# The attention mask's corner set before its load, and a dense tile's experts copied by VectorE ahead of the next search

## The chip, the cores and the metric

One core of one Trainium2 chip runs the whole program. The metric is the device time of one execution in microseconds (us), the median of three runs. The profile shows one further execution, recorded by the hardware profiler.

## The reference, cut to what matters

One layer of a streaming encoder over 512 positions of width 1024 (fp32):

```python
z = rmsnorm(x) @ w_in                    # x_lru, gate, q, k, v
y_a = rg_lru(x_lru) * gelu(gate)         # conv, gates, scan over positions
y_b = chunk_attention(q, k, v, rel_bias) # 8 heads; a chunk of 64 sees itself and 8 before it
x = x + concat(rmsnorm(y_a), rmsnorm(y_b)) @ w_out
x = x + memory_cross_attention(...)      # 4 heads, 256 memory tokens
# PEER: 8 heads, 128 x 128 = 16384 single-neuron experts, 16 picked per head
v1, i1 = top_k(q1 @ keys1, 16); v2, i2 = top_k(q2 @ keys2, 16)
top, pos = top_k(v1[:, None] + v2[None, :], 16)
idx = (i1 * 128 + i2)[pos]; g = softmax(top)
out = (g * gelu(x @ expert_u[idx])) @ expert_v[idx]
return rmsnorm(x + out)
```

In the attention the scores of a block of 128 queries get the relative-position bias added, and a key of a later chunk gets -1e30. In a tile of 128 queries by 512 keys that is one corner: the first 64 queries against the last 64 keys.

## The kernel before

All positions lie in four tiles of 128. Every fp32 product is made of three matmuls on a value's high and low part; the weights are split on the chip (a copy on ScalarE, L169, and a subtraction on VectorE, L207; for some of the U weights the low part is made by a ScalarE copy, L175, and an accumulating DMA from the POOL queue, L176).

A planner turns the program text into one fixed queue for each engine: it takes the instruction that stands first by its priority (the place in the text, moved forward by `tc.high_priority(offset=...)`) among those that its own model of time holds ready. `tc.issue_after(ins)` ties what a block traces, on the engine of `ins`, to come behind `ins` in that queue. On the chip each engine runs its queue strictly in order, and waits where an input or a buffer isn't there. From the last stage on (`tc.manual_schedule()`) the order is that of the text.

**The mixing stage** follows the string MIX_ORDER. Three letters bear on the change. "B" is `load_bias(h)` (L558 to L561): the bias of head h is loaded from HBM into a tile bt of 128x512 by one DMA on the SP queue (L560), and VectorE then writes -1e30 into the corner `[0:64, 448:512]` (L561), so that this memset waits for the load. "S" is `scores(h)`: two matmuls for each query tile (L573, L574) and one VectorE operation that adds bt and takes the maximum (L575). "R" is `lru_rec(n)` (L532 to L537), a row of VectorE operations of the recurrence on what ScalarE left from the gates (L520 to L524). The value projection `z_v` keeps four PSUM banks (pv) until ScalarE and VectorE have taken high and low part of each out of it (L106, L107).

**The expert stage.** The first query tile, t = 0, is done by gathering its experts. Tiles 1 to 3 are dense: for each token a table of 128x128 weights is built, one for each pair of key indices, and the experts are then computed for all tokens. `second_level(t, tp)` is the search that picks the 16 experts of each head for tile t: it is a generator, and each `yield` ends a step. The first step makes the candidate sums (L1001 to L1005); then come maxima and their positions (L1013 to L1023), an exponential on ScalarE (L1028), two passes over eq (L1050 to L1063), and the weights gF (L1068 to L1070). At its end PE turns the picked indices and weights into a PSUM bank pt (L1082, L1084). ScalarE copies the indices out to ij (L1089) and the scaled weights to gg[:, :, 0] (L1090), and VectorE makes gg's low part from both (L1091).

Search 1 runs beside eight blocks of the first expert product (`mm1_parts`, 24 matmuls each, L112 to L114). Then tile_ = 1, 2, 3 are built, 16 groups each: VectorE makes hot (L1125, from ij) and wei (L1129, from hot and gg), each with two buffers; PE multiplies them in two halves of 8 matmuls (L1136), ScalarE takes each half out into a stage (L1138), and a stage goes to DRAM (Wd, L1148). Between the halves PE gets parts of further U blocks by a fixed rate, and the text takes two steps of the search for tile_ + 1 in every three halves (`level`, offset OFF2 = 10). At a later point gathers, the second product (L1241) and the rest of the U blocks run by hand-written order.

Of the kernel before, what the change touches and what calls it, by code (L numbers as in the profile page):

```python
# [16 lines left out]
AF = mybir.ActivationFunctionType  # L17
OP = mybir.AluOpType
# [37 lines left out]
GS = float(2 ** 15)  # L56
# [20 lines left out]
def layer(ctx, tc, a, out, upto=99, dbg=None):  # L77
    nc = tc.nc
    dbg = dbg or {}
    V, A, PE, SP, PL = nc.vector, nc.scalar, nc.tensor, nc.sync, nc.gpsimd  # L80
# [12 lines left out]
    def bank(name="bk"):  # L93
        return psum.tile([128, 512], F32, name=name, tag="bk")
# [242 lines left out]
    def s(name, dt=F32):  # L337
        return s1.tile([128, S], dt, name=name, tag="s")
# [216 lines left out]
    BT, PR, PT, PO = {}, {}, {}, {}  # L555
    LAST = []

    def load_bias(h):  # L558
        BT[h] = s("bt")
        SP.dma_start(BT[h], a["bias"][h])  # L560
        V.memset(BT[h][0:64, 448:512], NEG)  # L561

    def scores(h):
        b, hs = divmod(h, 2)
        q, kh, kl = QK[b][hs], QK[4 + b][hs], QK[4 + b][2 + hs]
        mx = sm.tile([128, TT], F32, name="mx")
        su = sm.tile([128, TT], F32, name="su")
        P = PR[h] = [s("p") for t in range(TT)]
        for qt in range(TT):
            n = (qt + 1) * 128  # L570
            qs = slice(qt * 128, (qt + 1) * 128)
            ps = bank()
            PE.matmul(ps[:, :n], q[:, qs], kh[:, :n], start=True, stop=False)  # L573
            PE.matmul(ps[:, :n], q[:, qs], kl[:, :n], start=False, stop=True)  # L574
            V.tensor_tensor_reduce(P[qt][:, :n], ps[:, :n], BT[h][:, 512 - n:], scale=1.0, scalar=LOW,  # L575
                                   op0=OP.add, op1=OP.max, accum_out=mx[:, qt:qt + 1])
        V.tensor_scalar(mx, mx, -1.0, None, op0=OP.mult)
        for qt in range(TT):
            n = (qt + 1) * 128
            with tc.issue_after(LAST[-1]) if LAST else ExitStack():  # L580
                e = A.activation(P[qt][:, :n], P[qt][:, :n], AF.Exp, bias=mx[:, qt:qt + 1], accum_out=su[:, qt:qt + 1]).ins
        if h == 3 or h == 4:
            LAST[:] = [e] * 4
        return su
# [91 lines left out]
    for n in range(4):  # L676
# [3 lines left out]
    kinds = {"q": z_qk, "k": lambda n: z_qk(4 + n), "v": z_v, "gt": z_gate, "mk": mem_k, "mv": mem_v}  # L680
    steps = {
        "B": load_bias, "G": lru_gates, "R": lru_rec, "A": lambda n: lru_act(), "L": lru_scan,
        "W": lambda n: kinds[MIX_W[n][0]](MIX_W[n][1]),
        "S": lambda h: su.update({h: scores(h)}), "P": lambda h: probs(h, su[h]), "T": turn, "V": values,
# [164 lines left out]
    with tc.tile_pool(name="hx", bufs=2) as hx:  # L849
        ho = []  # L850
        for c in range(NCH):
            t = hx.tile([128, S], F32, name="ht")
# [36 lines left out]
    def mm1_next():  # L889
        ahead[0] += 1  # L890
        return mm1_parts(ahead[0] - 1)
# [77 lines left out]

    Wd = dram.tile([128, 8 * DT, NE, 16], F32)  # L970
    HK = [128, 8, 16]
    SEL = {}

    class Rooms:

# [20 lines left out]
    def second_level(t, tp):  # L996
# [89 lines left out]
        ij = tp.tile([128, 16, 2, 8], F16, name="ij", bufs=2)  # L1086
        gg = tp.tile([128, 16, 2, 8], F16, name="gg", bufs=2)
        pv = pt.rearrange("p (s g k) -> p s g k", s=4, k=8)
        A.copy(ij.rearrange("p g s k -> p s g k"), pv[:, 0:2])  # L1089
        A.activation(gg[:, :, 0], pv[:, 2], AF.Copy, scale=GS)  # L1090
        V.scalar_tensor_tensor(gg[:, :, 1], pv[:, 2], GS, gg[:, :, 0], op0=OP.mult, op1=OP.subtract)  # L1091
        SEL[t] = ij, gg

    def hurried(steps, offset):
        while True:
            with tc.high_priority(offset=offset) if offset else ExitStack():
                if next(steps, 0) == 0:
                    return
            yield

    with (tc.tile_pool(name="wg", bufs=2) as wg, tc.tile_pool(name="st", bufs=2, side="right") as stages,
          tc.tile_pool(name="wx", bufs=1) as W.more):
        parts, owed = iter(()), 0.0
        done = 0
        for k, _ in enumerate(hurried(second_level(1, tp), OFF1)):
            while ahead[0] < LAG and done < (k + 1) * U_MID / 15 and done < U_MID:
                done += 1
                for _ in mm1_next():
                    pass
        for tile_ in range(1, TT):  # L1110

            blocks = U_TILE[tile_ - 1] if tile_ < DT else LAG - SPARE - ahead[0]
            rate = blocks * NCH / 16
            level = hurried(second_level(tile_ + 1, tp) if tile_ < DT else iter(()), OFF2)
            ij, gg = SEL.pop(tile_)
            for q in range(8):
                tb = (tile_ - 1) * 8 + q
                stage = stages.tile([128, NE, 16], F32, name="stage", tag="stage")
                for t8 in range(0, 16, 8):
                    gr = (q * 16 + t8) // 8  # L1120

                    pairs = lambda x: x[:, gr].rearrange("p s (q k) -> p (s q) k", k=2)
                    F8 = [128, 8, NE, 2]
                    hot = wg.tile(F8, F16, name="hot")
                    V.tensor_tensor(hot, io2[:, None].to_broadcast(F8), pairs(ij)[:, :, None].to_broadcast(F8),  # L1125
                                    op=OP.is_equal)
                    wei = wg.tile(F8, F16, name="wei")
                    W8 = [128, 2, 4, NE, 2]
                    V.tensor_mul(wei.rearrange("p (s q) n k -> p s q n k", s=2),  # L1129
                                 hot[:, None, 0:4].to_broadcast(W8),  # L1130
                                 gg[:, gr].rearrange("p s (q k) -> p s q k", k=2)[:, :, :, None].to_broadcast(W8))
                    for t4 in (0, 4):
                        ps = bank()
                        for k in range(t4, t4 + 4):
                            for part in range(2):
                                PE.matmul(ps[:, (k - t4) * 128:(k - t4 + 1) * 128], hot[:, 4 + k // 2, :, k % 2],  # L1136
                                          wei[:, 4 * part + k // 2, :, k % 2], start=part == 0, stop=part == 1)
                        A.activation(stage[:, :, t8 + t4:t8 + t4 + 4], ps.rearrange("p (t i) -> p i t", t=4),  # L1138
                                     AF.Copy, scale=1.0 / GS)
                        if (q * 4 + (t8 + t4) // 4) % LEVEL[1] < LEVEL[0]:  # L1140
                            next(level, 0)
                        owed += rate / 2
                        while owed >= 1:
                            owed -= 1
                            if next(parts, 0) == 0 and ahead[0] < LAG - SPARE:
                                parts = mm1_next()
                                next(parts)
                SP.dma_start(Wd[:, tb], stage)  # L1148
            for _ in level:
                pass  # L1150
        for _ in parts:
            pass
        while ahead[0] < LAG - SPARE:
            for _ in mm1_next():
                pass
        W.more = None
        W.fill(W.used + 3)
# [139 lines left out]
    order.enter_context(tc.manual_schedule())  # L1297

    level = second_level(0, Rooms(gp))

    def level_steps(n):
# [114 lines left out]
```

## Time and profile before

| | us |
|---|---|
| median of 3 runs | 1620.49 |
| lowest, highest | 1618.95, 1622.12 |
| the profiled execution | 1620.74 |
| its span, first to last instruction | 1618.7 |

The page of the profile gives busy times by engine, the span in 40 slices, and the groups of instructions. PE is TensorE's matmul, PEld its weight load, DVE VectorE, ACT ScalarE, POOL GpSimd, SP SyncE. In a timeline a row gives the start, the duration, the engine, the line, the operation, out<-in, shapes and a count; the bracket holds the idle time of the engine just before it and what ended that. Where an operation starts before the one ahead of it has ended, both overlap in the engine's pipeline. The granted clock of TensorE (PEclk) is 1.00 at 2.4 GHz and 0.50 at 1.2 GHz.

### The profile page before, as it was taken

The numbers are of one execution on the slowest core, as the hardware profiler recorded it, in microseconds if no ns is written. First come the engines' busy times: TensorE is split into PE (matmuls) and PEld (weight loads), VectorE is DVE, ScalarE is ACT, GpSimd is POOL, SyncE is SP. The second block draws the span as 40 slices with busy tenths as digits, with TensorE's granted clock in tenths as the row PEclk, the third lists the DMA queues.
The fourth block names the chain that finished last, engine by engine and source line by source line (L and its number), as shares of the span: only waits on it lengthen the run. The fifth ranks groups of instructions, "written<-read, shape, count | busy, mean of one in ns | idle before, by whom it ended". The sixth has DMA issues, their size and how long they took to land.

```text
span 1618.7 us, 23682 instructions
## 1 busy us (share of the span) xinstructions
PE 1590.8 (98%) x8554; PEld 1402.6 (87%) x8554; DVE 1259.5 (78%) x2444; ACT 748.8 (46%) x1192; POOL 458.6 (28%) x335
## 2 busy tenths in 40 slices
PE   9999999999998999999999999999999999999998
PEld 7788878888887989899999999999999999988886
DVE  6778884655899986887777777777777777788887
ACT  6578753446545666553333333333333333333335
POOL 0111000001101100003454455454445454553330
PEclk9999999999999999999999999999999999999999
DMA  7454442127867789877999889889898998999994
GB/s 247 143 136 130 139 157 92 66 66 212 201 150 179 229 254 299 286 248 265 323 311 319 313 309 320 294 317 317 302 328 304 319 315 298 324 326 335 315 333 156
DMA packets 156933, 403.73 MB, mean 249 GB/s; under 512 B 13856, under 2 KB 64672, under 8 KB 153744
## 3 DMA queue, kind: packets, MB, share of 16 engines
q1 hardware_dynamic: 111744, 242.10, 43.5%
q0 software_dynamic: 44928, 159.86, 32.0%
q8 instruction: 67, 1.10, 0.3%
q14 instruction: 50, 0.41, 0.1%
q10 hardware_dynamic: 144, 0.26, 0.0%
HBM read 348.69 MB, written 29.36 MB: 234 GB/s over the span
## 4 chain that ended last, share of the span: by engine, by line
PE 87%; DVE 7%; DMA 3%; ACT 3%; issue 1%; SPq 0%; POOL 0%; ACTq 0%; DVEq 0%; POOLq 0%
PE acc L1241 33%; PE bk L112 15%; PE bk L114 15%; PE bk L113 15%; PE bk L1136 2%; DMA Wd<-stage 2%; PE om L113 1%; PE om L114 1%; PE om L112 1%; PE bk L932 1%; PE pv L112 1%; PE pv L113 1%; DVE wl L207 1%; PE pv L114 1%; DVE hot L1125 1%
## 5 line engine op out<-in xcount | busy, mean ns | idle before, releaser
L169 ACT CAST wh<-w 128x1024 fp32r<-128x1024 f32 x326 | 342.5, 1051 | 305.2 <-PE acc L1241 193.4
L112 PE MATMUL bk<-hH,wh 128*128 128x384 f32 (+1 forms) x1096 | 383.0, 349 | 0.0
L114 PE MATMUL bk<-hH,wl 128*128 128x384 f32 (+1 forms) x1096 | 374.7, 342 | 0.0
L113 PE MATMUL bk<-hL,wh 128*128 128x384 f32 (+1 forms) x1096 | 374.2, 341 | 0.0
L207 DVE TENSOR_TENSOR wl<-w,wh 128x1024 fp32r<-128x1024 f32 x286 | 348.8, 1221 | 20.7 <-ACT wh L169 20.2
L1170 POOL DMA_INDIRECT g<-in_Un,gidx x128 | 205.6, 1606 | 238.7 <-DVE junk L1177 193.7
L1170 POOL DMA_INDIRECT g<-in_V,gidx x128 | 199.7, 1560 | 226.8 <-DVE gacc L1187 211.4
L1241 PE MATMUL acc<-wh,ph 128*128 128x512 f32 x768 | 239.3, 391 | 0.0
L1241 PE MATMUL acc<-wh,pl 128*128 128x512 f32 x768 | 238.8, 391 | 0.0
L1241 PE MATMUL acc<-wl,ph 128*128 128x512 f32 x768 | 238.7, 390 | 0.0
L1217 DVE TENSOR_TENSOR pl<-act,ph 128x384 fp32r<-128x384 f32 x128 | 71.2, 557 | 185.8 <-ACT ph L1214 185.8
L113 PEld LDWEIGHTS bk<-hL,wh 128*128 128x128 f32 x1096 | 206.4, 188 | 7.0
L112 PEld LDWEIGHTS bk<-hH,wh 128*128 128x128 f32 x1096 | 206.2, 188 | 7.0
L114 PEld LDWEIGHTS bk<-hH,wl 128*128 128x128 f32 x1096 | 206.0, 188 | 4.1
L880 ACT ACTIVATE act<-bk 128x384 f32<-128x384 f32 x128 | 62.9, 491 | 281.0 <-PE bk L114 277.9
L176 POOL DMA_DIRECT2D wl<-w x40 | 34.3, 857 | 485.3 <-ACT wl L175 432.8
L1241 PEld LDWEIGHTS acc<-wl,ph 128*128 128x128 f32 x768 | 144.1, 188 | 31.8 <-DVE wl L207 0.3
L1241 PEld LDWEIGHTS acc<-wh,pl 128*128 128x128 f32 x768 | 144.1, 188 | 31.1
L1241 PEld LDWEIGHTS acc<-wh,ph 128*128 128x128 f32 x768 | 142.9, 188 | 24.3
L1187 DVE SCALAR_TENSOR_TENSOR gacc<-g,gu,gacc 128x1024 f32<-128x1024 f32 x127 | 162.5, 1279 | 1.6 <-DMA g<-in_V,gidx 0.9
L1177 DVE SCALAR_TENSOR_TENSOR junk<-g,htok 128x1024 bf16<-128x1024 f32 x128 | 156.1, 1220 | 1.0
L112 PE MATMUL bk<-oh,wh 128*128 128x512 f32 x280 | 112.4, 402 | 1.4 <-DVE v L107 1.4
(348 smaller groups left out, 2177.8 us busy)
## 6 DMA issues: line engine op xcount, KB each, us to landing
w<-in_V SPq DMA_DIRECT2D x128, 512.0 KB
w<-in_U SPq DMA_DIRECT2D x124, 512.0 KB
Wd<-stage SPq DMA_DIRECT2D x24, 1024.0 KB
wt<-Wd SPq DMA_DIRECT2D x90, 256.0 KB
wl<-w POOLq DMA_DIRECT2D x40, 512.0 KB
w<-in_w_pq SPq DMA_DIRECT2D x16, 512.0 KB
w<-in_w_in SPq DMA_DIRECT2D x14, 512.0 KB
x<-in_xT SPq DMA_DIRECT2D x16, 256.0 KB
```

What stands on the lines that cost most here:

```text
L112: PE.matmul(ps, lh, rh, start=first and c == 0, stop=False)
L113: PE.matmul(ps, lh, rl, start=False, stop=False)
L114: PE.matmul(ps, ll, rh, start=False, stop=last and c == n - 1)
L169: A.copy(wh[:, cs], w[:, cs])
L176: PL.dma_start(wl, w, accum_op=OP.add)
L207: V.tensor_sub(wl[:, cs], w[:, cs], wh[:, cs].bitcast(F32))
L880: A.activation(ACT[e], ps[:, :ND], AF.Gelu_apprx_tanh)
L1170: PL.indirect_dma_start(out=g, out_offset=None, in_=a[table], in_offset=bass.IndirectOffsetOnAxis(ap=gidx[:, k:k + 1], axis=0))
L1177: V.scalar_tensor_tensor(junk, g, 1.0, htok, op0=OP.mult, op1=OP.mult, accum_out=gu[:, st:st + 1])
L1187: V.scalar_tensor_tensor(gacc, g, gu[:, k:k + 1], gacc, op0=OP.mult, op1=OP.add)
L1217: V.tensor_sub(PS[e][1], ACT.pop(e), PS[e][0].bitcast(F32))
L1241: PE.matmul(acc[t, hf], lhs[:, ts], rhs[:, hf * 512:(hf + 1) * 512], start=e == 0 and part == 0, stop=e == NE - 1 and part == 2)
```

## The change

Two edits.

In `load_bias` the memset of the corner comes first in the text, and the load of the bias becomes two DMAs that leave the corner out: columns 0 to 447 of all 128 partitions, and columns 448 to 511 of partitions 64 to 127. No load writes what the memset writes.

In `second_level`, for t = 1 alone, ij and gg[:, :, 0] are copied out of PSUM by VectorE. The low part of gg, the last VectorE operation of the search, is kept in FOUND. The search for tile 2, which the loop of tile 1 takes its steps from, is wrapped in `behind`: its first step is traced as it was, and of all further steps what runs on VectorE is queued behind FOUND[1].

```diff
     def load_bias(h):
         BT[h] = s("bt")
-        SP.dma_start(BT[h], a["bias"][h])
+
         V.memset(BT[h][0:64, 448:512], NEG)
+        SP.dma_start(BT[h][:, :448], a["bias"][h][:, :448])
+        SP.dma_start(BT[h][64:128, 448:512], a["bias"][h][64:128, 448:512])
...
-    SEL = {}
+    SEL, FOUND = {}, {}
...
-        A.copy(ij.rearrange("p g s k -> p s g k"), pv[:, 0:2])
-        A.activation(gg[:, :, 0], pv[:, 2], AF.Copy, scale=GS)
-        V.scalar_tensor_tensor(gg[:, :, 1], pv[:, 2], GS, gg[:, :, 0], op0=OP.mult, op1=OP.subtract)
+        if t == 1:
+
+            V.tensor_copy(ij.rearrange("p g s k -> p s g k"), pv[:, 0:2])
+            V.tensor_scalar(gg[:, :, 0], pv[:, 2], GS, None, op0=OP.mult)
+        else:
+            A.copy(ij.rearrange("p g s k -> p s g k"), pv[:, 0:2])
+            A.activation(gg[:, :, 0], pv[:, 2], AF.Copy, scale=GS)
+        FOUND[t] = V.scalar_tensor_tensor(gg[:, :, 1], pv[:, 2], GS, gg[:, :, 0], op0=OP.mult, op1=OP.subtract).ins
         SEL[t] = ij, gg
...
+    def behind(steps, ins):
+
+        if next(steps, 0) == 0:
+            return
+        yield
+        while True:
+            with tc.issue_after(ins):
+                if next(steps, 0) == 0:
+                    return
+            yield
...
             level = hurried(second_level(tile_ + 1, tp) if tile_ < DT else iter(()), OFF2)
+            if tile_ == 1:
+                level = behind(level, FOUND[1])
```

## Rows read from the trace of the kernel before

**Rows 1.** The page: PE's busy time, share and instructions, and its busy tenths in 40 slices of the span.

```profile
PE 1590.8 (98%) x8554; PEld 1402.6 (87%) x8554; DVE 1259.5 (78%) x2444; ACT 748.8 (46%) x1192; POOL 458.6 (28%) x335
...
PE   9999999999998999999999999999999999999998
```

**Rows 2.** The list of waits of PE over the whole span, the longest: who waited for whom, us in total, times, the longest.

```profile
PE bk L1136 <- DVE wei L1129: 10.2, 5, 8.0
...
PE bk L573 <- DVE v L107: 2.0, 1, 2.0
```

**Rows 3.** Busy time of each engine in stretches of the span, with the granted clock, the DMA engines' share and GB/s as the last three columns.

```profile
80.00:90.00 10.00, 10.00 (x40) 8.17 (x40) 8.29 (x20) 4.62 (x11) 3.73 (x8) 0.83 0.44 123
...
210.00:220.00 10.00, 8.75 (x41) 6.60 (x41) 9.80 (x19) 6.35 (x11) 0.00 (x0) 1.00 0.17 56
...
520.00:530.00 10.00, 6.41 (x43) 6.04 (x44) 9.26 (x11) 4.26 (x6) 0.00 (x0) 0.66 0.56 145
530.00:585.00 55.00, 54.45 (x454) 49.26 (x453) 53.20 (x122) 36.81 (x57) 5.99 (x7) 1.00 0.85 252
585.00:640.00 55.00, 55.00 (x458) 50.17 (x457) 36.35 (x31) 34.08 (x54) 5.14 (x6) 1.00 0.92 286
```

**Rows 4.** VectorE's timeline from 60 to 76 us.

```profile
69.16 0.11 DVE L561 MEMSET bt<- 64x64 f32 x1 [5.77 <-DMA bt<-in_bias]
69.30 0.69 DVE L532 SCALAR_TENSOR_TENSOR ti<-ti,xc 128x512 f32<-128x512 f32 x1
...
74.72 0.48 DVE L107 SCALAR_TENSOR_TENSOR v<-pv,rmix,v 128x256 fp32r<-128x256 f32 x1
```

**Rows 5.** ScalarE's timeline from 60 to 85 us.

```profile
64.65 0.82 ACT L524 ACTIVATE T<-T,sp 128x512 f32<-128x512 f32 x1
...
69.77 0.47 ACT L106 ACTIVATE v<-pv,rmix 128x256 fp32r<-128x256 f32 x1
```

**Rows 6.** PE's timeline from 74 to 85 us (eleven matmuls start from 78.81 to 83.21 us, both counted).

```profile
76.37 0.61 PE L573 MATMUL bk<-qk,qk 128*128 128x512 f32 x1 [2.00 <-DVE v L107]
...
78.81 0.77 PE L112 MATMUL bk<-oh,wh 128*128 128x512 f32 x1 [1.40 <-DVE v L107]
...
83.21 0.47 PE L113 MATMUL bk<-ol,wh 128*128 128x512 f32 x1
...
84.22 0.39 PE L114 MATMUL bk<-oh,wl 128*128 128x512 f32 x1
84.45 0.39 PE L112 MATMUL bk<-oh,wh 128*128 128x512 f32 x1
```

**Rows 7.** What the SP queue's load of the bias (L560) waited for from 55 to 230 us, the longest: us in total, times, the longest.

```profile
SPq L560 <- DVE mo L107: 3.5, 1, 3.5
```

**Rows 8.** VectorE's timeline around the fourth head's mask, 105 to 125 us.

```profile
119.55 0.11 DVE L561 MEMSET bt<- 64x64 f32 x1
...
120.42 0.29 DVE L575 CUSTOM_DVE_ANT_0 p<-bk,bt 128x128 f32<-128x128 f32 x1
```

**Rows 9.** VectorE's timeline from the end of search 1 to the first group of tile 1 (494 to 530 us).

```profile
508.05 0.67 DVE L1013 MAX8 tops<-cand 128x8 f32<-128x80 f32 x4
...
519.86 0.27 DVE L1091 SCALAR_TENSOR_TENSOR gg<-bk,gg 128x128 f16<-128x128 f32 x1
520.05 2.35 DVE L1125 TENSOR_TENSOR hot<-io,ij 128x2048 f16<-128x2048 f16 x2
522.32 2.35 DVE L1129 TENSOR_TENSOR wei<-hot,gg 128x2048 f16<-128x2048 f16 x2
```

**Rows 10.** ScalarE's timeline from 512 to 530 us.

```profile
516.76 1.06 ACT L175 ACTIVATE wl<-w 128x1024 fp32r<-128x1024 f32 x1 [4.41 <-DMA w<-in_U]
517.72 0.35 ACT L1089 CAST ij<-bk 128x256 f16<-128x256 f32 x1
```

**Rows 11.** PE's timeline from 495 to 530 us: the last instruction that fills pt, the last matmul of the eighth U block, and the first and third half of tile 1.

```profile
511.31 0.28 PE L1084 MATMUL bk<-ident,gF 128*128 128x128 f32 x1
...
515.28 0.34 PE L114 MATMUL bk<-hH,wl 128*128 128x384 f32 x1
523.59 1.01 PE L1136 MATMUL bk<-wei,hot 128*128 128x128 f16 x8 [7.97 <-DVE wei L1129]
...
528.84 0.64 PE L1136 MATMUL bk<-wei,hot 128*128 128x128 f16 x8
```

**Rows 12.** PE's timeline, halves of tile 1 further on: the fifth, sixth, seventh and tenth, and the thirtieth.

```profile
533.06 0.64 PE L1136 MATMUL bk<-wei,hot 128*128 128x128 f16 x8
534.66 0.64 PE L1136 MATMUL bk<-wei,hot 128*128 128x128 f16 x8
536.76 0.64 PE L1136 MATMUL bk<-wei,hot 128*128 128x128 f16 x8
...
542.58 0.64 PE L1136 MATMUL bk<-wei,hot 128*128 128x128 f16 x8
...
584.42 0.64 PE L1136 MATMUL bk<-wei,hot 128*128 128x128 f16 x8
```

**Rows 13.** VectorE's timeline, the first and the last operation of search 3 before its weights are turned (530 to 592 us).

```profile
537.92 0.24 DVE L1001 TENSOR_TENSOR cand<-val 128x128 f32<-128x128 f32 x1
...
579.62 0.69 DVE L1063 TENSOR_TENSOR half<-eq 128x1024 f16<-128x1024 f16 x1
```

**Rows 14.** The tile ij: ScalarE's copies into it, duration in ns (lowest, median, highest), first and last start.

```profile
L1089 ACT CAST ij<-bk x3: 355/363/372, 517.7 to 638.4; 128x256 f16<-128x256 f32 x3
```

## The prediction

> **What bounds the kernel now.** I read the page first. PE is busy 98% of the span, 27.9 us short of all of it, and one slice, the thirteenth, falls to 8 tenths [rows 1]. So the time can only come down where PE stands still or runs at the lower clock. The list of PE's waits says where: 10.2 us, of which one wait is 8.0, for VectorE's wei ahead of the first product of the dense tiles, and a wait of 2.0 us for VectorE's v in the mixing stage [rows 2]. Then the stretches: in 80 to 90 us the granted clock is 0.83, in 520 to 530 us 0.66, and 1.00 in the others shown, also in 210 to 220 where PE stood 1.25 us of ten [rows 3]. So the change aims at two places, and I follow each through the timelines of VectorE, ScalarE and PE.
>
> **Edit one, the mask.** VectorE stood 5.77 us until 69.16 because its memset waited for the bias load, and the recurrence (L532 onward) and v's low parts were queued behind it [rows 4]. ScalarE had finished what the first step of the recurrence needs at 64.65 + 0.82 = 65.5 us, and the first high part of v at 69.77 + 0.47 = 70.2 us [rows 5]. With the memset first, no wait for a load stands in VectorE's queue. The recurrence starts as ScalarE delivers, and its operations ahead of v, about 5.4 us in the old order [rows 4], lie under ScalarE's gates. VectorE's first v can then start at about 70.3 instead of 74.72: 4.4 us sooner.
>
> What PE pays now is a wait of 2.00 at 76.37 and one of 1.40 at 78.81, both for v, whose PSUM banks it wants. On top come slow matmuls: eleven starts from 78.81 to 83.21 are 0.44 apart, against 0.23 from 84.22 to 84.45, ten times 0.21 = 2.1 us, and two more at 76.37, 0.4 us [rows 6]. The sum is 5.9 us. Moving v by 4.4 takes the first release from 76.3 to 71.9, ahead of PE, which wants it at 74.4; the second goes from 78.7 to 74.3, and PE, without its first wait and slow clock, would be there at about 75. So both waits and the fall of the clock go. But VectorE and ScalarE are only 4.4 us ahead, so PE may have to give back up to 1.5 us behind this. I take 4.9, half way between 4.4 and 5.9.
>
> What it adds: eight more DMA issues on SP, which nobody waits for, and nothing on VectorE, since the eight memsets of 0.11 [rows 4] only move. As the first writer of its buffer, though, the memset now has to wait for the buffer's last reader, which the load on SP did before. The nearest row is SP's longest such wait, 3.5 us for VectorE's own mo [rows 7]: in VectorE's own queue that is order and costs nothing. Bounds of the edit: a gain of 5.9, and a loss of 3.5 if such a wait for another engine falls on VectorE at a bad place. I stay near the gain, because the row of the longest wait names VectorE itself.
>
> The corner's DMA moves rows of 64 values, 256 bytes each. The mask is needed soonest for the fourth head: its memset found the load landed at 119.55, and the first read came at 120.42 [rows 8]. So there is a margin of 0.87 us or more, and a small second load can eat it at that head alone; I cost it at 0; the upper end is the one wait for a mask that the trace has, 5.77 [rows 4].
> The Trainium skill ("DMA: Bandwidth & Descriptors", the table at its head) asks for 512 B or more for full rate, and says that less is written by read-modify-write; by that the corner's load would be the late one, and the sum would go from 13.0 towards 13.0 - 5.8 = 7.2, instead of losing nothing to it. No row here shows a load of such short rows by itself.
>
> **Edit two, ij and gg on VectorE, search 2 behind.** PE fills pt by 511.31 + 0.28 = 511.6 us, and has no work of its own after the eighth U block, 515.28 + 0.17 = 515.45; then it stands 7.97 us, until 523.59 [rows 11]. In between pt lay waiting. ScalarE's queue held a U weight's low part ahead of ij, and that waited 4.41 us for its load, so that ij came at 517.72 [rows 10]. VectorE meanwhile did search 2 from 508.05 on, and came to gg's low part only at 519.86 [rows 9]. So two queues were late, ScalarE's by 6 us and VectorE's by 8; the change takes away both, and one alone would leave the other.
>
> After it VectorE, done with the first step of search 2 at 508.05, stands until pt is there. Then ij, gg and its low part. ScalarE's ij took 0.35 [rows 10], VectorE's low part, which also reads 128x128 out of pt, 0.27 [rows 9]; so 0.35 + 0.27 + 0.27 = 0.9 us, with 0.8 to 1.4 as ends (1.4 if ij, twice the elements and written out of order, costs thrice the low part). hot starts at 512.5. From the first hot to the first product it was 523.59 - 520.05 = 3.54 us with two hots ahead of two weis [rows 9, 11], and 2.4 if wei comes straight behind its hot (any two of them take 2.35). The first product can then start between 514.9 and 516.0, against PE's 515.45. I take a wait of 0.3 us. So 7.97 - 0.3 = 7.7 us go. The clock fell with the long stand: the first two halves took 528.84 - 523.59 = 5.25 us, and the same pair further on took 536.76 - 533.06 = 3.70 [rows 11, 12], 1.55 lost. A stand of 0.3 doesn't bring that, since 1.25 us in 210 to 220 left the clock at 1.00 [rows 3]. Together 9.2 us.
> The Trainium skill ("VectorE: DVE Perf Modes", Specifications) speaks against the move: ScalarE lies closer to PSUM, and VectorE to SBUF. The rows of this case don't bear that out for size: VectorE's read of pt took 0.27 for 128 columns and ScalarE's 0.35 for 256. If the move doubled the copies' 0.6 us, the sum would be 0.6 us smaller, 12.4 instead of 13.0.
>
> What is pushed back is VectorE's work of 508.05 to 519.86, 11.8 us of search 2 [rows 9]. It now lies among tile 1's groups. There PE is full: four halves take 542.58 - 534.66 = 7.92 us, so a group of two halves 3.96 [rows 12]. VectorE's hot and wei take 2.3 of that [rows 9]. The other 1.7 were filled before too, since VectorE was busy 53.2 of 55 us, but by search 3, from 537.92 to 579.62 [rows 3, 13], whose ij is not copied before 638.4 [rows 14], a whole tile later. Search 2 takes that room, and search 3 goes on to tile 2, where VectorE had 55 - 36.35 = 18.7 us free [rows 3]. The 11.8 us are nine of a search's fifteen steps, 1.3 us each, and the first is done, so 14 steps take 18 us. The room is about 16 x 1.7 = 27 us a tile, part of it for the low parts of U weights, so it fits, though not evenly: two steps are asked for in three halves, 1.33 steps or 1.7 us a group, all of the room for as long as the search lasts. Some groups will come late. Before, from 534.66 to 584.42 the 24 halves took 49.76 where 24 x 1.98 = 47.5 would do: 2.2 us [rows 12]. I expect about 1 us more than that, with -2 to +4 as ends. So edit two gives 9.2 - 1 = 8.2, between 4.5 and 11.
>
> ScalarE loses two copies of 0.6 us together, and POOL's accumulating DMA, which stood behind that ScalarE queue, can only go sooner.
>
> **The sum.** 4.9 + 8.2 = 13.1, taken as 13.0 us. Against the profiled execution, 1620.74 us (span 1618.7 and 2.0 around it), that is 1607.7. The median of the runs is 0.25 lower, and I predict 1608. After the dense tiles PE is full and the order is written by hand, so what is gained ahead of it arrives at the end.
>
> **Rivals.**
> *The mask's gain is given back.* VectorE and ScalarE are busy eight tenths from 80 us on [rows 3], and a mask that is late, or a memset that stands for a buffer, can hold PE again before 200 us. For: the margin at the fourth head. Against: VectorE moves forward as well. Gain 0 to 2 and 8.2: 1610.5 to 1612.5, about 1612.
> *VectorE binds in tile 1 or 2.* If the pushed 11.8 us are put ahead of the next hots by the planner, PE waits where it was fed before, and of the 9.2 only 0 to 3 stay. For: 53.2 of 55 busy. Against: search 3 can wait. With 4.9 from the mask: 1613 to 1616.
> *Slower: the steps of a search delay PE one by one.* They stand 10 places forward in the text's order, so in tiles 1 and 2 a step may be queued ahead of a hot that PE wants. 28 steps of some 1.3 us are at stake; from 0.47 us of each uncovered, 13 us, the change loses, and at 0.6, 17 us, the time is about 1624. Against: before, steps of search 3 lay in the same places and cost 2.2 us in all.
> *It doesn't do what it says.* If the parts of one tile aren't told apart, the loads wait for the memset, and if pt is turned later in PE's queue, nothing is won: 1620.5.
>
> **How the numbers follow.** Forecast, 1605 to 1611: 0.60. Mask given back, about 1612: 0.14. VectorE binds, 1613 to 1617: 0.12. Slower: 0.07. Nothing: 0.07. The range goes from 1604 (all 15 us and part of the old 2.2) to 1615, and leaves out some 0.2. A measurement can tell 0.2%, 3.2 us, from no change. Faster by more: 0.60 + 0.14 + 0.12, less 0.02 at the edge, 0.84. Within: 0.09. Slower: 0.07.
>
> **What would show it.** Right: no wait of VectorE's memset for a load; VectorE's first v near 70; the granted clock 1.00 in 80 to 90 and 520 to 530; VectorE's ij at 511.6 less the 5 us of edit one; the first L1136 less than 1 us behind the last U matmul; search 3 ending after tile 2 has begun. Wrong: PE waiting again for v, for masked scores or for hot in tiles 1 and 2, or VectorE's memset waiting for PE or ScalarE.

## The result and the profile after

The changed kernel took 1609.19 us in the median of 6 runs (1608.58 to 1610.49), the kernel before beside it 1619.74 (1618.72 to 1622.12): a ratio of 0.9933, 95% interval 0.9921 to 0.9946. The profiled execution took 1609.12 us with a span of 1607.1, against 1620.74 and 1618.7 before, so in the traces 11.6 us are to be explained.

The page after, PE's line and its slices, as in [rows 1]; then the list of PE's longest waits, as in [rows 2].

```profile
PE 1588.7 (99%) x8554; PEld 1402.7 (87%) x8554; DVE 1258.9 (78%) x2446; ACT 749.0 (47%) x1190; POOL 459.0 (29%) x335
...
PE   9999999999999999999999999999999999999998
```

```profile
PE bk L1156 <- DVE wei L1149: 3.8, 6, 1.8
PE po L613 <- ACT ph L102: 2.7, 1, 2.7
```

PE's busy time is 2.1 us smaller and the span 11.6: what went is mostly standing (9.5 us), the rest is slow clock. The thirteenth slice is full now. The wait of 8.0 for wei has become six of 1.8 at most, the waits for v are gone from the list, and the wait for ScalarE's ph has grown, from two of 1.0 at most to one of 2.7. The stretches, as in [rows 3]:

```profile
70.00:80.00 10.00, 10.00 (x48) 8.27 (x47) 8.68 (x19) 6.11 (x12) 2.08 (x4) 1.00 0.42 125
80.00:90.00 10.00, 10.00 (x52) 8.43 (x51) 8.65 (x25) 9.19 (x24) 2.06 (x4) 1.00 0.71 177
140.00:150.00 10.00, 7.27 (x49) 6.92 (x48) 6.78 (x12) 9.30 (x22) 1.03 (x2) 0.86 0.50 129
500.00:510.00 10.00, 10.00 (x70) 9.76 (x69) 6.38 (x16) 6.93 (x9) 2.57 (x3) 1.00 0.74 150
510.00:520.00 10.00, 10.00 (x88) 9.12 (x87) 10.00 (x35) 5.77 (x9) 0.86 (x1) 1.00 0.90 219
520.00:530.00 10.00, 9.75 (x79) 8.82 (x76) 10.00 (x43) 8.17 (x12) 1.71 (x2) 1.00 0.98 287
530.00:540.00 10.00, 9.57 (x81) 8.74 (x80) 10.00 (x13) 6.81 (x11) 0.06 (x1) 1.00 0.95 339
540.00:575.00 35.00, 34.07 (x282) 30.45 (x280) 33.30 (x99) 21.88 (x36) 4.23 (x5) 1.00 0.93 261
575.00:600.00 25.00, 23.20 (x179) 21.27 (x178) 24.79 (x30) 16.28 (x26) 1.71 (x2) 0.93 0.77 253
600.00:630.00 30.00, 30.00 (x256) 27.04 (x255) 19.12 (x18) 19.08 (x31) 3.42 (x4) 1.00 1.00 287
```

The two places the change aims at, 80 to 90 and 520 to 530 us, run at a granted clock of 1.00 (0.83 and 0.66 in [rows 3]). VectorE is all but full from 510 to 600 us (1.9 us free of 90), and PE stands 1.8 us between 575 and 600 and runs part of that time at the lower clock.

VectorE's timeline at the head, as in [rows 4], and at the start of tile 1, as in [rows 9]:

```profile
63.14 0.19 DVE L561 MEMSET bt<- 64x64 f32 x2
63.65 0.69 DVE L532 SCALAR_TENSOR_TENSOR ti<-ti,xc 128x512 f32<-128x512 f32 x1 [0.32 <-ACT ti L521]
...
69.97 0.49 DVE L107 SCALAR_TENSOR_TENSOR v<-pv,rmix,v 128x256 fp32r<-128x256 f32 x1
...
506.25 0.42 DVE L1093 CAST ij<-bk 128x256 f16<-128x256 f32 x1 [3.62 <-PE bk L1086]
506.60 0.28 DVE L1094 TENSOR_SCALAR gg<-bk 128x128 f16<-128x128 f32 x1
506.79 1.21 DVE L1145 TENSOR_TENSOR hot<-io,ij 128x2048 f16<-128x2048 f16 x1
507.92 0.28 DVE L1098 SCALAR_TENSOR_TENSOR gg<-bk,gg 128x128 f16<-128x128 f32 x1
508.28 1.21 DVE L1149 TENSOR_TENSOR wei<-hot,gg 128x2048 f16<-128x2048 f16 x1
```

The memset waits for nothing, and v's low part starts 4.75 us sooner than at 74.72. The copy of ij starts as soon as pt is there; one hot and one wei stand between it and the first product. PE's halves, as in [rows 11, 12] (the first and the third half, the thirtieth, three in tile 2), and behind the tiles the first product with V:

```profile
510.08 0.64 PE L1156 MATMUL bk<-wei,hot 128*128 128x128 f16 x8
...
513.78 0.64 PE L1156 MATMUL bk<-wei,hot 128*128 128x128 f16 x8
...
570.43 0.64 PE L1156 MATMUL bk<-wei,hot 128*128 128x128 f16 x8
...
582.82 0.64 PE L1156 MATMUL bk<-wei,hot 128*128 128x128 f16 x8 [1.80 <-DVE wei L1149]
...
585.55 1.08 PE L1156 MATMUL bk<-wei,hot 128*128 128x128 f16 x8
...
588.58 0.64 PE L1156 MATMUL bk<-wei,hot 128*128 128x128 f16 x8
...
709.05 0.63 PE L1261 MATMUL acc<-wh,ph 128*128 128x512 f32 x2
```

In the trace before, the counterparts of the half at 588.58 and of the first product with V:

```profile
598.68 0.64 PE L1136 MATMUL bk<-wei,hot 128*128 128x128 f16 x8
...
720.67 0.63 PE L1241 MATMUL acc<-wh,ph 128*128 128x512 f32 x2
```

The first half starts with no wait, 13.5 us before its counterpart at 523.59, the third 15.1 before 528.84, and the thirtieth 14.0 before 584.42. In tile 2 the lead shrinks: the half at 588.58 leads its counterpart by 10.1. About 2 us of the loss went with the wait of 1.80, and 1.5 between there and 588.58, where PE ran in part at the lower clock (eight matmuls took 1.08 at 585.55, where 0.64 is usual; the granted clock from 582.8 to 588.6 is 0.71). By the first product with V the lead is 11.6, and it stays so to the end. So 5 us of lead were lost in the tiles, nearly 4 of them after the thirtieth half, and 1.5 came back.

### The profile page after: what moved, and what is told of

The parts are those of the page before. It is cut to its first block, busy times and chain, and to the rows that moved or that the text cites. A ratio compares the mean times of both kernels' runs of the same rounds, so it can differ in the third digit from the quotient of the medians.

```text
span 1607.1 us, 23704 instructions
## 1 busy us (share of the span) xinstructions
PE 1588.7 (99%) x8554; PEld 1402.7 (87%) x8554; DVE 1258.9 (78%) x2446; ACT 749.0 (47%) x1190; POOL 459.0 (29%) x335
## 4 chain that ended last, share of the span: by engine, by line
PE 90%; DVE 6%; DMA 2%; ACT 1%; issue 1%; SPq 0%; DVEq 0%; ACTq 0%
PE acc L1261 33%; PE bk L112 16%; PE bk L113 16%; PE bk L114 16%; DMA Wd<-stage 2%; PE bk L1156 1%; DVE wei L1149 1%; DVE hot L1145 1%; PE om L112 1%; PE om L113 1%; PE om L114 1%; PE bk L934 1%; DVE wl L207 1%; PE pv L114 1%; PE pv L113 1%; PE pv L112 1%
## 5 line engine op out<-in xcount | busy, mean ns | idle before, releaser
L1190 POOL DMA_INDIRECT g<-in_Un,gidx x128 | 205.8, 1608 | 238.8 <-DVE junk L1197 194.8
```

The costliest lines, as they stand in the source:

```text
L1190: PL.indirect_dma_start(out=g, out_offset=None, in_=a[table], in_offset=bass.IndirectOffsetOnAxis(ap=gidx[:, k:k + 1], axis=0))
```

## The experiments

Each kernel is told as an edit of the kernel before or of the changed one. Two measures are used. The times are set against the kernel before, run beside it on the same chip; runs of one kernel scatter by 2 to 6 us. The second is a length inside one profiled execution, from the last row of sixteen products of the first-level scores (L932, or L934 where two lines were added) to the first product with V. It holds only the dense tiles and what leads into them, so what scatters earlier in the program is left out. That scatter is large: over the twelve executions with the mask edit the last score stands between 471.7 and 476.6 us. Two executions of the changed kernel gave 235.5 and 235.8 for it, and two of the one with two steps ahead 233.8 both times.

| kernel | median us | less than before | last score | first half | first V | stretch |
|---|---|---|---|---|---|---|
| before | 1619.74 | 0 | 478.89 | 523.59 | 720.67 | 241.8 |
| changed | 1609.19 | 10.6 | 473.52 | 510.08 | 709.05 | 235.5 |
| changed, again | 1609.55 | 11.1 | 475.31 | 511.88 | 711.08 | 235.8 |
| mask alone | 1616.08 | 4.3 | 471.94 | 518.41 | 715.67 | 243.7 |
| memset on GpSimd | 1615.25 | 4.6 | 473.94 | 520.32 | 716.87 | 242.9 |
| copies and order, old mask | 1613.42 | 7.0 | 479.69 | 518.20 | 718.08 | 238.4 |
| mask, copies, no order | 1613.06 | 7.3 | 476.57 | 520.13 | 717.91 | 241.3 |
| mask, order, no copies | 1615.81 | 4.6 | 473.09 | 515.11 | 715.50 | 242.4 |
| no search 3 | 1606.97 | 12.9 | 475.06 | 511.62 | 706.03 | 231.0 |
| two steps ahead | 1606.98 | 12.8 | 473.07 | 510.08 | 706.87 | 233.8 |
| two steps ahead, again | 1607.14 | 13.5 | 473.21 | 510.22 | 707.03 | 233.8 |
| three steps ahead | 1608.55 | 11.3 | 473.39 | 511.94 | 709.28 | 235.9 |
| low parts later | 1608.72 | 11.9 | 471.72 | 508.28 | 707.27 | 235.6 |
| two steps, low parts later | 1608.99 | 11.6 | 473.02 | 510.04 | 710.40 | 237.4 |

**The mask alone** (edit of the kernel before):

```diff
-        SP.dma_start(BT[h], a["bias"][h])
         V.memset(BT[h][0:64, 448:512], NEG)
+        SP.dma_start(BT[h][:, :448], a["bias"][h][:, :448])
+        SP.dma_start(BT[h][64:128, 448:512], a["bias"][h][64:128, 448:512])
```

> The kernel before with the new load of the mask and nothing else. Theory (each edit gives on its own; the mask edit frees VectorE's queue at the head and its 5.1 to 5.4 us are kept to the end): 1614.5 us, 1613.5 to 1615.5, with the v tile of L107 at about 70 us instead of 74.7 and the first half of the first dense tile at about 518 instead of 523.6. Rival (the 5 us are lost again at a later wait unless the second edit is there): 1618 to 1620.

1616.08, ratio 0.9973 (0.9962 to 0.9983): 4.3 us gained, 2.8 to 6.2. That is 0.6 above the range of the theory and 1.9 below the rival's. The last score stands 7.0 us earlier in this execution, but the stretch behind it is 1.9 us longer. ScalarE's timeline, beside [rows 10], and then the end of VectorE's wait, beside [rows 9], say why:

```profile
513.13 1.06 ACT L175 ACTIVATE wl<-w 128x1024 fp32r<-128x1024 f32 x1 [6.77 <-DMA w<-in_U]
514.10 0.35 ACT L1091 CAST ij<-bk 128x256 f16<-128x256 f32 x1
```

```profile
514.66 0.29 DVE L1093 SCALAR_TENSOR_TENSOR gg<-bk,gg 128x128 f16<-128x128 f32 x1 [0.69 <-ACT gg L1092]
```

The low part that stands ahead of ij waited 6.77 us for its load instead of 4.41: the last score had come forward by 7.0 us and this low part, 516.76 before, by 3.6. VectorE was done with its part of search 2 at 513.97, 5.9 us sooner than before, and then stood 0.69 us for ScalarE. So of the 1.9 us about 0.7 were held by ScalarE's queue and 1.1 by VectorE's own, and the second edit takes both queues out of the way.

**The memset on GpSimd** (edit of the kernel before; the old load of the whole mask stays):

```diff
-        V.memset(BT[h][0:64, 448:512], NEG)
+        PL.memset(BT[h][0:64, 448:512], NEG)
```

> The kernel before with its old load of the whole mask, and the corner's memset on GpSimd's queue instead of VectorE's. Theory (edit one gains because VectorE's queue no longer stands behind a transfer; the bytes left out and the second request count for nothing): as the mask edit alone, 1615 to 1616.5, v of L107 at about 70 us. Rival (the smaller load, or the order in which VectorE's work falls, is what gains): 1619 to 1621.

1615.25, ratio 0.9969 (0.9954 to 0.9984), as the mask alone. GpSimd's timeline, then VectorE's v:

```profile
68.39 0.18 POOL L561 MEMSET bt<- 64x64 f32 x1 [5.04 <-DMA bt<-in_bias]
```

```profile
69.96 0.48 DVE L107 SCALAR_TENSOR_TENSOR v<-pv,rmix,v 128x256 fp32r<-128x256 f32 x1
```

The wait of 5 us is still there, now in GpSimd's queue, and v starts at 69.96 as with the split load. So edit one gains by freeing VectorE's queue; the bytes left out are worth nothing that can be seen.

**Copies and order, old mask** (the changed kernel, with the three lines of the first diff turned back):

> The changed kernel with the old load of the mask (whole tile, then the corner's memset behind it). Theory: 1609.2 + 5.2 = 1614.4 us; against the kernel before, 9.7 us gained ahead of the third half and 3 to 4 of them given back by the end of the tiles, net 5 to 6.5, so 1613.5 to 1615. Rival (the give-back in tiles 1 and 2 has the size of the whole lead, mask and copies together, since a stage behind binds): the copies alone give back less, 1611 to 1612.5.

1613.42, ratio 0.9958 (0.9944 to 0.9972): 7.0 us gained, 0.1 below the theory's range and 0.9 above the rival's. With the mask's 4.3 that is 11.3, against 10.6 and 11.1 for both: by the times the edits add up within their scatter, and the size of the give-back isn't settled by this run. Its profiled execution was the slowest of its six (1618.17), so its row in the table is a poor measure of the stretch.

**No order** (the changed kernel):

```diff
-            if tile_ == 1:
-                level = behind(level, FOUND[1])
```

> The changed kernel (mask and VectorE's copies) without the order that puts the next tile's search behind. Theory (the order is what lets VectorE copy at once): VectorE is inside the search when the PSUM tile fills, its two copies start 6 to 7 us later, the first product is at about 517 instead of 510.1 and the clock falls to half in the gap; some of that is not given back later, so 1612.5 to 1615. Rival (the copies on VectorE alone do it, the order is idle): 1609.2, first product within 1 us of 510.

1613.06, ratio 0.9955 (0.9941 to 0.9969), as the theory had it. Here too the profiled execution was the slowest of its five (1618.01), so its stretch may be too long. pt was full at 508.99 + 0.28 = 509.3 us. VectorE's timeline shows the copies behind the search's steps, up to 515.86:

```profile
514.72 1.22 DVE L1054 TENSOR_TENSOR eq<-rc,mio 128x2048 f16<-128x2048 f16 x1
515.86 0.42 DVE L1093 CAST ij<-bk 128x256 f16<-128x256 f32 x1
```

**No copies** (the changed kernel, both copies on ScalarE again):

```diff
-        if t == 1:
+        if t == 99:
```

> The changed kernel (mask and the order behind) with ScalarE's two copies back. Theory (ScalarE's queue, with a low part of U that waits for its load at its head, holds the copies): ij at 512.5 to 513, first product near 516, 6 us later than in the changed kernel, at half clock at first, and the search still late: 1614 to 1617. Rival (the order alone gives the gain, whoever copies): 1609.2 to 1610.

1615.81, ratio 0.9969 (0.9958 to 0.9980): also as the theory had it, no better than the mask alone. Now VectorE is free and waits for ScalarE; its timeline, then ScalarE's:

```profile
512.36 1.22 DVE L1145 TENSOR_TENSOR hot<-io,ij 128x2048 f16<-128x2048 f16 x1 [10.15 <-ACT ij L1096]
```

```profile
511.01 1.06 ACT L175 ACTIVATE wl<-w 128x1024 fp32r<-128x1024 f32 x1 [4.46 <-DMA w<-in_U]
511.97 0.35 ACT L1096 CAST ij<-bk 128x256 f16<-128x256 f32 x1
```

Against the mask alone (243.7) the stretch is 2.4 us shorter with the copies alone, 1.3 with the order alone, and 8.2 with both. Two queues held the same instruction, and each part alone leaves it in the other. The times say the same: 3.0, 0.3 and 6.3 to 6.8 us less than the mask alone.

**No search 3** (the changed kernel; tile 3 uses the experts and weights of tile 2, so this kernel leaves out a part of the layer):

```diff
-            level = hurried(second_level(tile_ + 1, tp) if tile_ < DT else iter(()), OFF2)
+            level = hurried(second_level(tile_ + 1, tp) if tile_ < 2 else iter(()), OFF2)
...
-            ij, gg = SEL.pop(tile_)
+            ij, gg = SEL.pop(tile_) if tile_ < 3 else (ij, gg)
```

> The changed kernel without the search of the last dense tile (its experts and weights are those of the tile before it, so its output differs there). Theory (the part of the lead that is given back between 540 and 600 us is VectorE's: it is full there with the two late searches beside the experts' products): the 3.5 us net of give-back stay, 1605 to 1606.5, with PE full between 575 and 600 us. Rival (they are lost to ScalarE's queue, to transfers or to the clock, whatever VectorE does): 1608.5 to 1610.

1606.97, ratio 0.9914 (0.9898 to 0.9930), 0.5 above the theory's range and 1.5 below the rival's: the times alone don't decide. The stretch speaks for the theory. It is 4.6 us shorter than the changed kernel's. About 1.4 of that is PE's own turning of search 3's result, which is left out too (16 products in 1.07 and a transpose of 0.28 when search 1 is turned); the other 3 are left for waits and clock. The stretch of the loss:

```profile
575.00:600.00 25.00, 25.00 (x204) 22.96 (x202) 17.26 (x15) 15.43 (x24) 2.35 (x3) 1.00 0.90 308
```

PE is full and at 1.00, and VectorE has 7.7 us free where it had 0.2.

**Two and three steps ahead** (the changed kernel, with 2 and with 3 for n; it has 1):

```diff
-        if next(steps, 0) == 0:
-            return
-        yield
+        for _ in range(n):
+            if next(steps, 0) == 0:
+                return
+            yield
```

> The changed kernel, but two steps of the next tile's search instead of one stand ahead of the copies; the second is four maxima and four index searches, 1.9 us, and VectorE stands idle 3.6 us there. Theory (VectorE's work sets the pace up to 600 us, so work done in its idle time comes off the give-back): first product still at 510, 1.0 to 1.9 us less in the end, 1607.3 to 1608.2. Rival (the give-back is a collision at one place and not VectorE's load): 1609.2.

> The same with three steps ahead: 1.9 and 2.1 us of the search against 3.6 us of idle time, so the copies start 0.4 us later. Theory: 2 to 3.6 us less of the give-back, less 0.4 at the first product, 1606 to 1607.6. Rival: 1609.2 to 1609.6.

> The changed kernel once more, as the measure for the three beside it on the same chip: 1608.5 to 1610.

> The changed kernel with two steps of the search ahead of the copies, beside the changed kernel on one chip. Theory (VectorE's 1.9 us in its idle time come off the give-back): 1 to 2 us below the changed kernel. Rival (the 2.2 us of the run on the other chip were scatter): within 0.5 us of it.

With two steps 1606.98, ratio 0.9917 (0.9901 to 0.9932), and again, beside the changed kernel's 1609.55 on one chip (1608.5 to 1610 expected), 1607.14, ratio 0.9916 (0.9902 to 0.9930). That is 2.4 us less than the changed kernel, somewhat more than expected; the stretch is 1.7 to 2.0 us shorter, as expected. The repeated run's VectorE timeline and one stretch:

```profile
503.50 0.24 DVE L1017 FIND_INDEX8 pos<-tops,cand 128x8 uint32<-128x80 f32 x1
505.80 0.43 DVE L1093 CAST ij<-bk 128x256 f16<-128x256 f32 x1 [2.07 <-PE bk L1086]
```

```profile
575.00:600.00 25.00, 24.15 (x197) 21.88 (x195) 23.56 (x25) 15.23 (x23) 2.57 (x3) 1.00 0.79 246
```

The second step fits into VectorE's idle time, the copies are not later, and PE loses 0.85 us in this stretch where it lost 1.80 and, in the second execution of the changed kernel, 2.54; its waits for wei are 2.5 us in all, 3.8 and 5.3 in the changed kernel. With three steps it was 1608.55, ratio 0.9923 (0.9906 to 0.9940), between the theory's range and the rival's, with an interval that covers both. The stretch, 235.9, is no shorter than the changed kernel's and speaks against the theory. The third step ran past the filling of pt, and ij started at 507.51, 1.3 us later than in the changed kernel, not 0.4; the first half came 38.6 us after the last score instead of 36.6. Of the versions that do the whole layer the one with two steps ahead has the lowest median; from three steps its distance is within the scatter.

**Low parts later** (the changed kernel), and **both** (two steps ahead as well):

```diff
-U_V = *range(11, LAG - U_DMA, 3), *range(LAG - U_DMA, LAG)
+U_V = 11, 17, 23, 26, 29, 31, 32, 34, 35, *range(LAG - U_DMA, LAG)
```

> The changed kernel with the low parts of two U blocks (14 and 20) given from VectorE to ScalarE and GpSimd's queue, and two of blocks in the last tile (31 and 34) to VectorE instead: VectorE has 2.4 us less before 600 us, and no step of a search is touched. Theory (VectorE's load is the pace there, of whatever kind): 1 to 2.4 us below the changed kernel, PE's waits for the weights tile shorter between 540 and 600 us. Rival (only where the search's steps stand counts): within 0.5 us of it.

> Two steps of the search ahead and the two low parts moved: 1.9 and 2.4 us taken from VectorE before 600 us. Theory: 2 to 4 us below the changed kernel, near 1606. Rival (once VectorE is relieved by either, PE is full): no better than the better of the two.

1608.72, ratio 0.9925 (0.9911 to 0.9938), and 1608.99, ratio 0.9921 (0.9906 to 0.9936): 0.8 and 0.6 us below the changed kernel, within the scatter. The first lies between the theory's range (1 to 2.4) and the rival's (0.5); the second is short of the 2 to 4 of its theory, and its median is above that of two steps alone, as the rival had it. The stretch is the changed kernel's (235.6), and with both it is 3.6 us longer than with two steps alone, in one execution that was 1.5 us above its median. So nothing here supports the theory that VectorE's load of whatever kind is the pace: 2.4 us less work for VectorE gave no clear gain. VectorE's timeline and ScalarE's in the first of the two:

```profile
556.05 1.23 DVE L207 TENSOR_TENSOR wl<-w,wh 128x1024 fp32r<-128x1024 f32 x1 [3.53 <-ACT wh L169]
```

```profile
551.98 1.06 ACT L175 ACTIVATE wl<-w 128x1024 fp32r<-128x1024 f32 x1 [5.90 <-DMA w<-in_U]
...
554.98 1.04 ACT L169 CAST wh<-w 128x1024 fp32r<-128x1024 f32 x1
```

ScalarE, with more low parts in its queue, waits 5.9 us for a load ahead of a high part, and VectorE's next low part stands 3.5 us for that high part, with the products' hot and wei queued behind. In the changed kernel that wait of VectorE's was 1.70. So most of what was taken off came back as a wait: 2.4 us less work, 1.8 us more waiting.

## Why the prediction came out as it did

**Predicted 1608, measured 1609.2, inside the range.** Two terms of the sum were near and one was too small: in the traces 5.4 + 9.7 - 3.5 = 11.6 us, where 4.9 + 9.2 - 1 = 13.1 was forecast. That the time came within 1.2 us is in part luck: the first two terms were each half a microsecond too small, and that hid a part of the 2.5 that the third was off.

**Edit one, 4.9 predicted.** v came at 69.97 (70.3 predicted), both waits of PE for v and the slow clock at 80 to 90 went. The recurrence's first step started at 63.65, when ti was there, and not at 65.5 as read from [rows 5]; v doesn't hang on it. The lower bound, a memset that waits for another engine, did not happen. Behind the two places PE leads by 6.4 us (its first product that turns the attention weights p, L600, stands at 86.85, at 93.29 before), of which 0.3 was there ahead of them: 6.1, against the 5.9 of the sum. At the last score it leads by 5.4 (by 3.6 in the second execution of the changed kernel, within the scatter told above). So about 1 us was given back on the way, inside the "up to 1.5" that the prediction allowed, and the rival of a gain given back before 200 us holds for no more than that. The place is PE's wait for ScalarE's ph, with the lower clock behind it (0.86 in 140 to 150):

```profile
146.66 0.50 PE L613 MATMUL po<-ph,v 128*128 128x512 f32 x1 [2.73 <-ACT ph L102]
```

The trace before has four waits there, between 151 and 167 us, of 1.00, 0.67, 0.94 and 0.26. A new wait of 1.25 at 167 us stands against two of 0.66 and 0.59 at 215 to 219 that are gone. Two things in the prediction don't hold as written: half way between 4.4 and 5.9 is 5.15 and not 4.9, and 9.2 with the ends of -2 and +4 gives 5.2 to 11.2 and not 4.5 to 11. With 5.15 the forecast would have been a quarter of a microsecond lower. What the prediction did not see is that a part of this lead needs edit two: with the mask alone, 1.9 us of it were lost again in the two queues ahead of the first dense tile.

**The corner's load, costed at 0, is confirmed.** The lines of the two loads (L562, rows of 448 values, 224 KB in all, then L563, the corner, 16 KB), from issue to landing:

```profile
DMA to landing us min/median/max: 2.3/3.5/6.1
```

```profile
DMA to landing us min/median/max: 2.2/3.2/6.0
```

The rule on short rows (the Trainium skill, "DMA: Bandwidth & Descriptors", Specifications) would have made the corner's load the late one; it was not. What short rows cost for each byte these lines can't say, since the corner's load moves a fourteenth of the bytes.

At the fourth head the corner was asked for at 110.47 and read at 113.08, with no wait.

**Edit two, the wait and the clock, 9.2 predicted.** The third half leads by 15.1, less the 5.4 of edit one: 9.7. The first product came at 510.08; 509.9 to 511.0 was predicted (514.9 to 516.0, less 5). The first two halves took 3.70 us, as the same pair did further on before, so the 1.55 of slow clock went too. ij took 0.42 and gg 0.28 on VectorE, against 0.35 predicted for ij from ScalarE's row. The statement that both queues were late and that one alone leaves the other is what the runs without the order and without the copies show.

**The give-back, 1 us predicted: the term that was mis-sized.** It measured 3.5 (9.7 less the 6.2 left at the first product with V), inside its ends of -2 and 4. For tile 1 the 1 us was right: 15.1 at the third half, 14.0 at the thirtieth. The step that failed is "Search 2 takes that room, and search 3 goes on to tile 2, where VectorE had 55 - 36.35 = 18.7 us free". The free time was counted over 55 us. But search 3 was not spread over them: its first step stands at 552.84, still in tile 1, and its last before the turning at 598.20, 21 us into tile 2. VectorE's timeline at the loss:

```profile
577.57 1.23 DVE L1054 TENSOR_TENSOR eq<-rc,mio 128x2048 f16<-128x2048 f16 x1
578.71 0.74 DVE L1045 TENSOR_TENSOR rc<-t,ov 128x128 f16<-128x128 f32 x1
579.05 1.45 DVE L1145 TENSOR_TENSOR hot<-io,ij 128x2048 f16<-128x2048 f16 x1
580.41 1.22 DVE L207 TENSOR_TENSOR wl<-w,wh 128x1024 fp32r<-128x1024 f32 x1
581.54 1.23 DVE L1149 TENSOR_TENSOR wei<-hot,gg 128x2048 f16<-128x2048 f16 x1
```

Two of its operations and a U low part stand ahead of one wei, and PE waits 1.80 for it at 582.82. In the second execution of the changed kernel the same wait comes again:

```profile
584.57 0.63 PE L1156 MATMUL bk<-wei,hot 128*128 128x128 f16 x8 [1.80 <-DVE wei L1149]
```

There it is followed not by a lower clock but by one more wait for wei, of 0.74. From 600 us on VectorE has 10.9 us free in 30, when search 3 is over (598 us). Without search 3 the loss is gone; with search 2 one step further on beforehand the stretch is 1.7 to 2.0 us shorter. So the rival "VectorE binds" was right in kind and too dear: it would have taken 6 to 9 of the 9.2 us, and 3.5 went. That PE's steps could be delayed one by one, the slower side, has the same mechanism; it never came near 13 us. Of the signs set down beforehand the right ones all came, search 3 ending in tile 2 among them, and one of the wrong ones as well: five of PE's six waits for wei lie in tiles 1 and 2, 3.4 us together.

What stays open: whether search 3, held back to where VectorE is free, would give the other 2 us as well. That wasn't tried. Nor is it settled whether the loss is VectorE's load or the place where a few operations fall: one step moved into idle time helped, and as much load taken off elsewhere did not.

## What to carry to other kernels

When a tile is late, list every queue that stands between its source and its reader: here ScalarE's and VectorE's both held it, each cure alone gave 0.3 to 3 us and the pair 6 to 7. Work pushed behind an urgent instruction must be placed, not only fitted: free time counted over a stage says little where a few steps fall between two products that PE waits for, and idle time just ahead of the urgent instruction can be filled, up to where it ends: a second step fitted here, a third made the copies 1.3 us late. Moving work to an engine whose queue waits for loads can bring the wait back through the next thing that engine owes.

## What was not expected of the hardware

The load of rows of 256 bytes (16 KB) landed hardly sooner than that of rows of 1792 bytes (224 KB) issued just before it: 3.2 against 3.5 us in the median, eight of each. And PE's clock did not follow the length of a stand alone: one of 2.73 at 146.66 left 0.86 in its stretch, one of 1.80 at 582.82 left 0.93 between 575 and 600, and the same 1.80 in the changed kernel's second execution left 1.00, as did stands of 0.25 to 0.68 between 520 and 575 us.
